# Attention scores over cached keys: one matmul against all heads, or each head in its own group of columns

## The chip, the cores and the metric

The kernel runs on one core of a Trainium2 chip. It is timed as device time in microseconds (us). One launch computes a whole inference step of a small decoder layer for two groups of tokens: 1024 prompt tokens, and 8 sample tokens, each with 256 cached keys of its own. Before the change the median of three runs is 1493.83 us (1492.7 to 1494.16).

## The reference

The layer is a mixer (four heads of differential attention beside four heads of retention, then one output projection), attention into a memory, and an MLP. The change touches one piece of the first: the differential attention of the 8 sample tokens.

```python
def probs(qi, ki):
    s = jnp.einsum('bqhd,bkhd->bhqk', qi, ki) * scale + bias
    return jax.nn.softmax(jnp.where(mask, s, neg), axis=-1)

attn = probs(q1, k1) - lam * probs(q2, k2)
return jnp.einsum('bhqk,bkhd->bqhd', attn, v)
```

A head has a query and a key of two halves of 64 (`q1`, `q2`, `k1`, `k2`), so two maps. For a sample token a map has 257 scores: 256 against its cached keys, which lie in pages of 128 keys at places that a page table names, and one against its own new key. A bias by distance, from a table of 32 rows and 4 heads, is added to each. In all there are 8 tokens x 4 heads x 2 maps = 64 rows of 257 scores. Everything is float32.

## The kernel before, in words

The program is one long list of instructions written by a Python function, `decoder_step`. A planner places it on the engines and adds the waits. Between `pin[0] = True` and `pin[0] = False`, matmuls keep the order in which the program writes them (`pinned`, `mm`, `transpose`); the other engines' order is the planner's, apart from places that name an instruction they must follow (`issue_after`, `behind`).

The stage around the change is the prompt's differential attention, head by head. A loop over `g` (line 1329), from -4 to 39, goes through ten items for each of the four heads. An item transposes a block of softmax weights (`turn`, `trA` in the trace), forms scores of one or two later blocks of 128 queries (`scores`, `sp`; the table `SCORES` says which, and `q` runs from 0 to 7), and multiplies the weights of the block before with the values (`weigh`, `av`). `scores` reads its banks with VectorE (line 1001, bias and running minimum), takes the exponential on ScalarE (line 1007) and combines the two maps on VectorE (line 1016, `e`). `turn` needs `e`, and `weigh` needs what ScalarE and VectorE made of the transpose (`ah`, `al`, lines 1034 and 1035).

Between these, other matmuls are dealt out by a generator, `filler`: `next(filler)` runs it to its next `yield`. It first yields the query and key projections of the heads to come (`head_proj`), then the sample tokens' attention (`decode_steps`). From item 28 on only the latter is left, and `DFILL` (line 2433) says how many turns of it each item from 28 to 39 takes: 1, 3, 4, 3, 1, 1, 2, 2, 1, 1, 1, 1. What is left runs out after the loop. From item 37 on, `out_ahead` adds matmuls of the output projection (`pr_o`).

`decode_steps` works so. Four of its turns are taken earlier by name (`DECODE_AT`): they load indices and constants and start the gathers of the first four of eight key tiles. A key tile (`raws2[4 * j + x]`, `ck` in the trace) is 128 partitions by 1024 columns: two tokens (`y`), four heads, 128 keys of page `j`; the partitions are the 128 elements of a key, both halves. A tile is two gathers of GpSimd's queue (`gather`, line 859). The first four tiles lie in buffers of the weight ring, the last four in the three buffers tagged `raw`, so they wait until these come free: the two from a row of factors and a block of values of the prompt's attention, and for the eighth tile that of the fifth. In the same queue item 30 puts two loads of 2 MB, `UL` and `UH` (`operand_steps`, line 1255), which the output projection needs.

The scores of one token, a step, are one matmul (line 1211): the stationary operand has 64 columns, the token's 8 queries (4 heads x 2 maps) in their own 8 columns and zeros in the others' 56; the moving operand is all 512 columns (4 heads x 128 keys) of that token. Eight tokens accumulate into one bank, 64 rows by 512 columns. Of each row only the 128 columns of its own head mean anything, so four VectorE instructions with a mask by head (line 1218, `hm`) pick them and add them to the bias rows in `SD`. The bias is a small matmul of its own (`dbias`), the own key's score another (`down`). A softmax over 257 columns follows, twelve turns that do nothing, and a matmul with `sel` that adds up the two maps (`dcomb`).

A float32 matmul shows in the trace as two weight loads and two matmuls, one for each pass.

## Time and profile before

| | before |
|---|---|
| device time, median of 3 runs | 1493.83 us |
| lowest and highest run | 1492.7, 1494.16 us |
| profiled execution | span 1492.5 us (the page gives no other time for it) |
| TensorE busy | 1474.0 us, 99% |
| VectorE, ScalarE, GpSimd busy | 1102.5, 678.4, 325.4 us |
| matmuls `dsc` (cached keys) | 32, from 397.4 to 435.7 us |

The span goes from the first instruction to the last of one profiled execution. TensorE is PE in the rows (its weight loads PEld), VectorE is DVE, ScalarE ACT, GpSimd POOL, and SP issues DMAs. Matmuls are pipelined: the duration of one is longer than the time until the next may start, so what a matmul costs is read from the start of one to the start of the next. In rows in order of time stand the start, the duration, engine, line, operation, what is written and read, the shape, how many were merged, and in square brackets how long the engine had been idle and what ended it.

### The profile page before, as it was taken

Reading aid. Unit: us, or ns where it says so; the run is one execution under the profiler, and the core shown is the slowest. Engines: PE = TensorE matmul, PEld = TensorE weight load, DVE = VectorE, ACT = ScalarE, POOL = GpSimd, SP = SyncE. Lnnn points to the kernel's source line nnn. Section 1 sums busy time; section 2 is a strip of 40 time slices with the busy share of each in tenths; the row PEclk is TensorE's granted clock in tenths of the full one; section 3 lists DMA queues with packets and bytes.
Section 4 is the critical chain, followed back from the end, with each engine's and each line's share of the span. In section 5 each row is a group of like instructions: output and inputs, shape, how many; then the busy total and the mean of one; then the engine's idle time right before and its main releaser. Section 6 shows DMA issues by size and latency. Waiting matters only on the chain.

```text
span 1492.5 us, 27826 instructions
## 1 busy us (share of the span) xinstructions
PE 1474.0 (99%) x10893; PEld 1402.5 (94%) x10893; DVE 1102.5 (74%) x2279; ACT 678.4 (45%) x1326; POOL 325.4 (22%) x346
## 2 busy tenths in 40 slices
PE   9999999998999999999999999999999999999997
PEld 7899779998769999989999999999999999999997
DVE  7656636987877734567786978888888889787875
ACT  7534435665652432147535634334344444343454
POOL 0035323114414321104132000000001311020380
PEclk9999999999999999999999999999999999999999
DMA  8155737214857157483592443344436674536273
GB/s 292 61 186 168 201 71 181 80 34 123 232 181 279 49 191 193 132 238 103 165 321 72 128 149 137 141 156 157 142 141 210 237 265 142 172 99 191 81 129 114
DMA packets 125229, 236.67 MB, mean 159 GB/s; under 512 B 13744, under 2 KB 76517, under 8 KB 124970
## 3 DMA queue, kind: packets, MB, share of 16 engines
q1 hardware_dynamic: 89056, 170.50, 36.5%
q0 software_dynamic: 24912, 44.80, 10.9%
q10 hardware_dynamic: 11130, 19.60, 3.5%
q8 instruction: 85, 1.39, 0.4%
q14 instruction: 46, 0.38, 0.1%
HBM read 170.24 MB, written 57.52 MB: 153 GB/s over the span
## 4 chain that ended last, share of the span: by engine, by line
PE 90%; DVE 5%; ACT 2%; issue 1%; DMA 1%; ACTq 0%; POOL 0%; DVEq 0%; SPq 0%
PE dn L2309 21%; PE Z L2143 9%; PE qkp L75 7%; PE pr_o L75 6%; PE mq L75 6%; PE pr_m L75 6%; PE X L2143 6%; PE Y L2143 6%; PE grp L75 3%; PE sp L75 2%; PE av L75 2%; PE mv L75 2%; PE mk L75 1%; PE mpv L75 1%; PE vap_z L522 1%
## 5 line engine op out<-in xcount | busy, mean ns | idle before, releaser
L2309 PE MATMUL dn<-UH,wd 128*128 128x258 f32 x1792 | 324.6, 283 | 0.0
L2309 PEld LDWEIGHTS dn<-UH,wd 128*128 128x128 f32 x1792 | 277.5, 189 | 0.7 <-ACT c L2410 0.2
L2309 PE MATMUL dn<-UL,wd 128*128 128x258 f32 x896 | 252.8, 282 | 0.0
L2309 PEld LDWEIGHTS dn<-UL,wd 128*128 128x128 f32 x896 | 169.0, 189 | 0.0
L2413 DVE TENSOR_TENSOR c<-c,dn 128x258 f32<-128x258 f32 x216 | 88.9, 418 | 38.5 <-PE dn L2309 36.1
L2169 ACT ACTIVATE hq<-r 128x258 f32<-128x258 f32 x128 | 53.7, 421 | 118.3 <-DVE r L2168 118.3
L2143 PE MATMUL Z<-T_h,wu 128*128 128x258 f32 x512 | 98.2, 284 | 0.0
L2143 PE MATMUL X<-UH,wu 128*128 128x258 f32 x512 | 97.4, 282 | 0.0
L2287 ACT CAST wd<-raw_d 128x512 fp32r<-128x512 f32 x96 | 58.8, 620 | 79.0 <-PE dn L2309 74.6
L1953 ACT CAST wu<-raw_up 128x512 fp32r<-128x512 f32 x96 | 59.1, 617 | 59.9 <-PE Z L2143 50.0
L2280 ACT CAST UH<-raw_h 128x1032 fp32r<-128x1032 f32 x56 | 58.7, 1056 | 53.5 <-PE dn L2309 27.7
L2143 PEld LDWEIGHTS X<-UH,wu 128*128 128x128 f32 x512 | 81.3, 188 | 0.2 <-ACT p L2194 0.2
L2143 PEld LDWEIGHTS Z<-T_h,wu 128*128 128x128 f32 x512 | 81.3, 189 | 0.0
L2180 POOL DMA_DIRECT2D HT<-ht x32 | 17.2, 538 | 292.3 <-DVE ht L2179 291.8
L2281 DVE TENSOR_TENSOR UL<-raw_h,UH 128x1032 fp32r<-128x1032 f32 x56 | 73.6, 1315 | 8.6 <-ACT UH L2280 8.6
L2288 DVE TENSOR_TENSOR wd<-raw_d,wd 128x512 fp32r<-128x512 f32 x96 | 72.2, 759 | 10.0 <-ACT wd L2287 9.9
L2143 PE MATMUL Z<-T_l,wu 128*128 128x258 f32 x256 | 72.3, 282 | 0.0
L2143 PE MATMUL X<-UL,wu 128*128 128x258 f32 x256 | 72.3, 282 | 0.0
L128 ACT CAST wh_u<-raw_u 128x1024 fp32r<-128x1024 f32 x43 | 44.6, 1047 | 54.3 <-PE mq L75 31.1
L1954 DVE TENSOR_TENSOR wu<-raw_up,wu 128x512 fp32r<-128x512 f32 x96 | 64.7, 687 | 3.5 <-ACT wu L1953 3.5
L2301 POOL TENSOR_TENSOR raw_d<-raw_d,raw_d 128x512 f32<-128x512 f32 x16 | 22.1, 1383 | 193.8 <-DVE raw_d L2297 172.9
L129 DVE TENSOR_TENSOR wl_u<-raw_u,wh_u 128x1024 fp32r<-128x1024 f32 x39 | 49.4, 1273 | 18.8 <-ACT wh_u L128 18.6
(597 smaller groups left out, 4732.8 us busy)
## 6 DMA issues: line engine op xcount, KB each, us to landing
raw_u<-in_wall SPq DMA_DIRECT2D x49, 512.0 KB
HT<-ht POOLq DMA_DIRECT2D x32, 516.0 KB
raw_h<-HT SPq DMA_DIRECT2D x32, 516.0 KB
raw_up<-in_wall SPq DMA_DIRECT2D x32, 512.0 KB
raw_d<-in_wall SPq DMA_DIRECT2D x32, 512.0 KB
HQ<-hq ACTq DMA_DIRECT2D x32, 387.0 KB
raw_h<-HQ SPq DMA_DIRECT2D x24, 516.0 KB
cmk<-in_cmk SPq DMA_DIRECT2D x16, 512.0 KB
```

The source lines that it names most:

```text
L75: pinned(nc.tensor.matmul(out, l, r, start=start, stop=stop))
L129: (lo_engine or nc.vector).tensor_sub(wl[:, :n], raw[:, :n], wh[:, :n].bitcast(F32))
L1953: nc.scalar.copy(w[:, :512], src)
L1954: nc.vector.tensor_sub(w[:, 512:], src, w[:, :512].bitcast(F32))
L2143: pinned(nc.tensor.matmul(ps, l, r[:, k, :], start=first and k == 0 and x == 0, stop=k == 3 and x == 2, skip_group_check=True))
L2169: nc.scalar.activation(h[:, PLACE[quad], :], r, AF.Square)
L2280: nc.scalar.copy(h, rv)
L2281: nc.vector.tensor_sub(l, rv, h.bitcast(F32))
L2287: nc.scalar.copy(w[:, :512], src)
L2288: nc.vector.tensor_sub(w[:, 512:], src, w[:, :512].bitcast(F32))
L2309: pinned(nc.tensor.matmul(ps, l, r[:, k, cq], start=first and k == 0 and x == 0, stop=k == 3 and x == 2, skip_group_check=True))
L2413: nc.vector.tensor_add(y, y, ps)
```

## The change

Each head now gets a matmul of its own. The 128 rows of one PSUM bank are split into four groups of 32, one for each head; a head's 16 columns (2 maps x 8 tokens) are the stationary operand, and its own 128 keys the moving one. The bank holds 257 columns, as many as a row has scores, and stays open from the first to the last matmul: a bias matmul starts it with half the bias, the own key's product goes into column 256, the eight tiles into columns 0 to 255, and a second bias matmul with the other half closes it. The softmax reads the bank itself. The steps `dec_bias`, the four masked instructions for each page and `hm` are gone, and `sel` and the mark of the second map lie in the tile `qk`. A `yield` now follows each tile instead of each token.

```diff
-            sel = A.tile([64, 32], F32, tag="sel", name="sel")
-            nc.sync.dma_start(sel, i["sel"])
-            hm = A.tile([64, 5], F32, tag="hm", name="hm")
-            nc.sync.dma_start(hm, i["hm"])
...
+            nc.vector.tensor_scalar(relw, relb.unsqueeze(2).to_broadcast([32, 4, 32]), 0.5, None, ALU.mult)
...
-            nc.gpsimd.memset(qx, 0.0)
+            prod = qk[:, 512:640]
+            nc.gpsimd.memset(qk[:, 0:640], 0.0)
...
+                nc.vector.tensor_mul(
+                    prod[ms].rearrange("p (h c) -> p h c", h=4)[:, :, 8 * m : 8 * m + 8], qdec[ms], kdec[ms])
...
+            sel, second = qk[:, 900:932], qk[:, 932:933]
+            nc.sync.dma_start(qk[:, 900:933], i["sel"])
...
-            def dec_bias():
-                bp = dt("dbias")
-                mm(bp[:64, :257], rel64, oneh, True, True)
-                nc.scalar.copy(SD[:, :257], bp[:64, :257])
-                yield
-                bp = dt("down")
-                for m in range(2):
-                    ms = slice(64 * m, 64 * m + 64)
-                    mm(bp[32 * m : 32 * m + 32, :1], prod[ms], ones[ms], True, True)
-                nc.vector.tensor_add(SD[:, 256:257], SD[:, 256:257], bp[:64, :1])
-                yield
+            sp = dt("dsc")
+            mm(sp[:, :257], relw.rearrange("p h c -> p (h c)"), oneh, True, False)
+            mm(sp[:, 256:257], prod, ones, False, False)
+            yield
 
             for j in range(2):
-                sp = dt(f"dsc_{j}")
                 for x in range(4):
                     raw = raws2[4 * j + x]
-                    if (j, x) == (0, 2):
-                        yield from dec_bias()
                     for y in range(2):
                         q = 2 * x + y
-                        mm(sp[:64, :], qx[:, q * 64 : q * 64 + 64], raw[:, y * 512 : y * 512 + 512], q == 0, q == 7)
-                        yield
+                        for h in range(4):
+                            pinned(nc.tensor.matmul(
+                                sp[32 * h : 32 * h + 16, j * P : j * P + P],
+                                qx[:, q * 64 + 16 * h : q * 64 + 16 * h + 16],
+                                raw[:, y * 512 + h * P : y * 512 + h * P + P],
+                                start=False, stop=False, skip_group_check=True))
+                    yield
 
                     if 4 * j + x in (0, 1, 2, 4):
                         fetch(4 + (0, 1, 2, 0, 3)[4 * j + x])
-                sd = SD[:, j * P : j * P + P]
-                for h in range(4):
-                    nc.vector.scalar_tensor_tensor(sd, sp[:64, h * P : h * P + P], hm[:, h : h + 1], sd, ALU.mult, ALU.add)
+            mm(sp[:, :257], relw.rearrange("p h c -> p (h c)"), oneh, False, True)
-            nc.vector.tensor_reduce(mn[:, 0:1], SD[:, :257], AX.X, ALU.min)
-            nc.scalar.activation(SD[:, :257], SD[:, :257], AF.Exp, bias=mn[:, 0:1], scale=-1.0, accum_out=mn[:, 1:2])
+            nc.vector.tensor_reduce(mn[:, 0:1], sp[:, :257], AX.X, ALU.min)
+            nc.scalar.activation(SD[:, :257], sp[:, :257], AF.Exp, bias=mn[:, 0:1], scale=-1.0, accum_out=mn[:, 1:2])
```

More of the change, by code (lines that the diff above doesn't have):

```diff
@@ L1186, in decode_steps @@
             nc.sync.dma_start(oneh, i["onehot_dec"])
[L1187 removed]
+            sel, second = qk[:, 900:932], qk[:, 932:933]
+            nc.sync.dma_start(qk[:, 900:933], i["sel"])
+            SD = A.tile([P, 260], F32, tag="SD", name="SD")
             yield
[L1191 to L1201 removed]
+            sp = dt("dsc")
@@ L1223, in decode_steps @@
+            mn = A.tile([P, 4], F32, tag="dmn", name="dmn")
+            nc.vector.tensor_reduce(mn[:, 0:1], sp[:, :257], AX.X, ALU.min)
+            nc.scalar.activation(SD[:, :257], sp[:, :257], AF.Exp, bias=mn[:, 0:1], scale=-1.0, accum_out=mn[:, 1:2])
             nc.vector.reciprocal(mn[:, 1:2], mn[:, 1:2])
-            nc.vector.tensor_scalar(mn[:, 2:3], nlam[:64], 1.0, None, ALU.subtract)
-            nc.vector.tensor_scalar(mn[:, 2:3], mn[:, 2:3], hm[:, 4:5], 1.0, ALU.mult, ALU.add)
+            nc.vector.tensor_scalar(mn[:, 2:3], nlam, 1.0, None, ALU.subtract)
@@ L1226, in decode_steps @@
+            nc.vector.tensor_scalar(mn[:, 2:3], mn[:, 2:3], second, 1.0, ALU.mult, ALU.add)
             nc.vector.tensor_mul(mn[:, 1:2], mn[:, 1:2], mn[:, 2:3])
```

26 lines of the change are left out of this document (9 added, 17 removed).

## The prediction

> **What bounds the kernel now.** I read the page first, then the busy times by stretch around the change, then the time-ordered rows of each engine there.
>
> ```profile
> span 1492.5 us, 27826 instructions
> PE 90%; DVE 5%; ACT 2%; issue 1%; DMA 1%; ACTq 0%; POOL 0%; DVEq 0%; SPq 0%
> ```
>
> The chain that ended last is TensorE for 90% of the span, so TensorE time taken out moves the end, wherever nothing else waits in its place. The page gives no device time for the profiled execution, only its span of 1492.5; I make the sum in the span's own clock. The median of the three timed runs, 1493.83, lies 1.3 above the span, and I add the change to that median. Busy time in a stretch where the cached keys are used, and in one behind it:
>
> ```profile
> 405.00:410.00 5.00, 5.00 (x24) 2.57 (x22) 4.30 (x14) 3.03 (x7) 1.54 (x4) 1.00 1.09 417
> 440.00:470.00 30.00, 30.00 (x190) 28.41 (x189) 15.12 (x32) 9.02 (x15) 7.69 (x6) 1.00 0.55 186
> ```
>
> After the length come the busy times of TensorE, its weight loads, VectorE (DVE), ScalarE and GpSimd, the clock, the DMA share and GB/s. Where the keys are used, VectorE is busy for 4.30 us of 5 and DMA for the whole time: TensorE leads by little, and two others stand close behind. Behind it, VectorE has half its time free. TensorE's own order, in start times (items are the values of `g` in the loop over the last head):
>
> ```profile
> 400.34 1.07 PE L75 MATMUL dsc<-ck,qblkd 128*64 128x512 f32 x2
> 401.35 0.39 PE L75 MATMUL av<-ah,VH 128*128 128x256 f32 x1
> 401.57 0.28 PE L75 MATMUL av<-al,VH 128*128 128x256 f32 x1
> 401.69 0.28 PE L75 MATMUL av<-ah,VL 128*128 128x256 f32 x1
> ...
> 406.68 0.64 PE L75 MATMUL dbias<-qblkd,rel 32*64 32x257 f32 x2
> 407.25 0.39 PE L75 MATMUL av<-ah,VH 128*128 128x256 f32 x1
> ...
> 408.15 0.23 PE L75 MATMUL down<-ones,qblkd 64*32 64x1 f32 x4
> 408.31 0.44 PE L75 MATMUL sp<-KA,Q 128*128 128x384 f32 x1
> ...
> 410.20 0.55 PE L78 MATMUL trA<-ident,e 128*128 128x128 f32 x3
> ...
> 411.68 0.47 PE L75 MATMUL sp<-KA,Q 128*128 128x448 f32 x1
> ...
> 427.11 0.55 PE L78 MATMUL trA<-ident,e 128*128 128x128 f32 x3 [0.38 <-DVE e L1016]
> ...
> 437.01 0.32 PE L75 MATMUL pr_o<-UH,wh_u 128*128 128x344 f32 x1
> ```
>
> Three marks carry the sum: 410.20, where item 31 begins; 427.11, the transpose that waits for the last prompt softmax (VectorE L1016); 437.01, the first output-projection matmul. Behind the third TensorE has ready work without a gap (the second row: busy for 30.00 of 30.00), so a shift there goes on to the end.
>
> **The matmuls.** One step (one of 16 rounds of a 512-column matmul in its two passes) takes 401.35 − 400.34 = 1.01 us. Sixteen are 16.2; the bias 407.25 − 406.68 = 0.57, the own key 408.31 − 408.15 = 0.16: 16.9 us go. In their place each key tile gets 2 rounds x 4 heads of 128 columns, two passes each. A pass of 512 columns is 1.01 / 2 = 0.50, of 128 columns 0.126. Side by side in four column groups, a tile is 2 x 2 x 0.126 = 0.5; the first step after a change of tile shape is 0.22 (401.35 to 401.57) against 0.12 for the next (to 401.69), so with 0.1 for that 0.6 us, eight tiles 4.8. Without overlap it is 16 x 0.126 + 0.1 = 2.1, eight tiles 16.8. No four column groups run in this trace; the nearest row is the own key, on two tiles of different rows and columns: four matmuls in 0.16 us, though each lasts far longer, and
>
> ```profile
> 408.15 0.19 PE L75 MATMUL down<-ones,qblkd 64*32 64x1 f32 x2
> 400.34 0.19 PEld L75 LDWEIGHTS dsc<-ck,qblkd 128*64 128x64 f32 x2 [0.19 <-issue]
> ```
>
> two of them lie within 0.19 us together, that is on top of each other (the first row is the answer for 408.155 to 408.203). I take 0.6, and keep 2.1 as the other end. The bias is now added twice, 1.14, the own key about 0.2 as before. Matmuls: 6.1 instead of 16.9, so 10.8 us less; without overlap 1.2 more. [...] The trace speaks against it: the two loads in the second row, on the same rows, are done in 0.19 us, while the first matmul, begun with the first load, runs for half a us.
>
> **Where the work stands.** The steps between yields get fewer: before, each 512-column step is one turn of the filler; now a whole tile is one, and bias and own key together are one. Items 28 to 39 still take 1, 3, 4, 3, 1, 1, 2, 2, 1, 1, 1, 1 turns (`DFILL`). So item 29 takes bias and tiles 0, 1; item 30 tiles 2 to 5; item 31 tiles 6, 7, the second bias and the softmax; items 32 to 37, which had 8 of the 16 steps, take none. The 10.8 us come out of the later items, while the need for tiles 4 to 7 moves forward from items 32 to 37 into items 30 and 31. TensorE's order is pinned: what waits for tile 6 holds up every score, transpose and value matmul behind it.
>
> **When the tiles land.** GpSimd issues, and DMA rate from 391 to 417 in 40 slices of 0.65 us:
>
> ```profile
> 400.68 0.82 POOL L1255 DMA_DIRECT2D UH<-OPH  x1
> 403.74 1.64 POOL L977 TENSOR_TENSOR VL<-vraw,VH 128x512 fp32r<-128x512 f32 x1 [2.24 <-ACT VH L975]
> ...
> 409.19 1.00 POOL L859 DMA_INDIRECT ck<-in_cache_kT,idk  x1 [0.51 <-POOL al L1033]
> 410.49 0.95 POOL L859 DMA_INDIRECT ck<-in_cache_kT,idk  x1 [0.30 <-issue]
> GB/s 139 180 251 330 298 197 227 157 209 167 297 380 419 419 413 393 386 392 405 405 411 405 404 404 410 424 413 432 432 426 432 406 406 386 341 139 25 25 0 0
> ```
>
> The gather of tile 6 (two issues, 409.19 and 410.49) stands in GpSimd's queue behind the load of UH; the bytes stop at 391 + 38 x 0.65 = 415.7. Its buffer is that of `vraw_3`, free once VL is made (403.74 + 1.64 = 405.4), so it can be issued 4 us sooner. That doesn't help: UH went out at 400.68, the rate is full until 413.7, and the same bytes stand ahead of it. Tile 6 is there at about 416, tile 7, two more gathers of 128 rows by 512 floats, 256 KB each, at some 0.4 MB per us, at 417.3.
>
> **Forward from item 31.** Items 29 and 30 hold 6 tiles, one bias and the own key, 3.6 + 0.8 = 4.4, where 5 steps, bias and own key took 5.8; their scores and transposes wait for VectorE, so I leave item 31 at 410.2, up to 1 sooner. Its transposes end at 410.7; tile 6 is due, and TensorE stands until about 416.0, 5.3 us. The scores of block 6 start at 416.6 instead of 411.68: 4.9 late. VectorE then has this to do until its last L1016:
>
> ```profile
> 412.40 0.62 DVE L1001 CUSTOM_DVE_ANT_0 e<-sp,M 128x448 f32<-128x448 f32 x1 [0.41 <-PE sp L75]
> ...
> 425.76 1.29 DVE L1016 SCALAR_TENSOR_TENSOR e<-e,mn,e 128x1024 f32<-128x1024 f32 x1
> L1218 DVE SCALAR_TENSOR_TENSOR SD<-dsc,hm,SD 64x128 f32<-64x128 f32 x4 | 1.3, 334 | 0.7 <-PE dsc L75 0.7
> 440.79 0.41 DVE L1220 TENSOR_REDUCE dmn<-SD 64x1 f32<-64x257 f32 x1
> ```
>
> 412.40 to 427.05 is 14.65. The four L1218 go (1.3) with the 0.7 waited for them; some 1.3 of it, block 5's L1016 (the row's 1.29 is that of the widest), gets done during TensorE's stand; the decode softmax comes in, its reduction 0.41 and three small ones, 1.1 at most. That leaves 12.4: from 416.6 + 0.7 to 429.7, so 427.11 becomes 429.7, 2.6 late. From there 9.9 us follow before, with 4 steps, 4.0, that are gone. TensorE alone would take 5.9; but VectorE has
>
> ```profile
> L129 DVE TENSOR_TENSOR wl_u<-raw_o,wh_u 128x1024 fp32r<-128x1024 f32 x3 | 3.7, 1221 | 0.0
> L145 DVE SCALAR_TENSOR_TENSOR UL<-op,subln,UH 128x1024 fp32r<-128x1024 f32 x2 | 2.6, 1282 | 0.2 <-ACT UH L144 0.2
> L1035 DVE TENSOR_TENSOR al<-trA,ah 128x512 fp32r<-128x512 f32 x3 | 2.1, 685 | 0.0
> ```
>
> (427.1 to 437.0), and ahead of the second L1035, which the value matmuls before 437.01 need, stand three L129, one L145 and one L1035: 3.7 + 1.3 + 0.7 = 5.7, with two small ones and that L1035 itself some 6.7, with the value matmuls behind it 7.6 in all. 429.7 + 7.6 = 437.3, or 436.1 if the third L129 falls behind it. I take 436.5, nearer the second, since VectorE's order is planned anew with less TensorE work in these items, against 437.01: 0.5 us earlier. Moved DMAs: `sel` now goes out on SP behind the one-hot rows, and the early loads of `sel` and `hm` are gone; nothing is queued close behind them. The four loads of output weights wait for the scores to end and come some 3 us later; they have until 437. All else in the diff (the wider memset, two products for one, a dropped copy on ScalarE) is under 0.3 us each on engines with room.
>
> **Forecast:** 1493.83 − 0.5 = 1493.3, own range 1490.8 to 1496.5: 2.5 less if both the third L129 falls behind and the tiles land a us sooner, 3 more if VectorE's order, which is planned anew, puts the decode softmax or the late `sel` in a prompt block's way.
>
> **Rivals.**
> *1. No stand.* If tile 6 is issued ahead of UH, it lands behind tile 5, by 411, and block 6 starts at 411.4. VectorE then bounds: 14.65 − 1.3 − 0.7 − 0.9 of waits on scores + 1.1 = 12.9 from 412.1, ends 425.0, plus 7.6 is 432.6: 4.4 earlier, less 0.4 for a partial wait, 1489.8. For it: the gather's place in the program moves from item 31 into item 30, ahead of both loads. Against: before, UL went out ahead of tile 5's gather though it stands behind it in the program, because the buffer wasn't free; tile 6's buffer frees later still.
> *2. Column groups in line: slower.* At 2.1 a tile, seven tiles, a bias and the own key (15.5) replace six steps, bias and own key (6.8) up to block 6's scores: 411.68 + 8.7, block 6 at 420, with nothing left to wait for from DMA. VectorE: 420.0 + 0.7 + 12.4 = 433.1, plus 7.6: 440.7, 3.7 late, 1497.5. It decides from some 1.5 us a tile, where TensorE reaches tile 6 after it has landed (410.7 + 6 x 0.9 = 416.1). Against it stand the two rows of overlap; for it, that no row has the same rows in four groups.
> *3. Clock falls in the stand.* Here the clock is 1.00 through waits as long as
>
> ```profile
> 359.87 0.55 PE L78 MATMUL trA<-ident,e 128*128 128x128 f32 x3 [2.03 <-DVE e L1016]
> 1486.00:1489.00 3.00, 0.00 (x0) 0.00 (x0) 2.37 (x4) 0.00 (x0) 0.00 (x0) 0.50 0.50 166
> ```
>
> 2.03 us, and 0.50 once TensorE is done at the end. 5.3 us lies between. At half clock for the first 3 us of work after it, block 6's and 5's work is up to 1.5 later: 1493.3 + 1.5 = 1494.8. [...]
>
> **Chances.** Forecast 0.48, rival 1 0.24, rival 2 0.18, rival 3 0.10. A change under 0.2%, 3 us, can't be told from none. Within it lie 0.41 of the forecast's 0.48 (0.04 faster, 0.03 slower), 0.02 of rival 1, 0.03 of rival 2 and 0.08 of rival 3: same 0.54, faster 0.04 + 0.22 = 0.26, slower 0.03 + 0.15 + 0.02 = 0.20. The range, 1488.5 to 1498.3, takes in rivals 1 and 2 up to a us beyond their values.
>
> **What would show it.** Weight loads of four heads starting a few ns apart, and a tile in 0.6 us, against 2.1; a TensorE wait of 4 to 6 us ahead of tile 6 that the gather ends; granted clock in that stretch; the 427.11 transpose 2 to 3 us later while the first output matmul is not. It is wrong if there is no such wait, or if the order of VectorE has changed so that the last L1016 ends before 427.

## The result, and the profile after

The change makes the kernel slower: 1501.07 us median (1500.1 to 1501.88, four runs) against 1493.59 (1492.7 to 1494.16, four runs), a ratio of 1.0046 with a 95% interval of 1.0032 to 1.0060. The profiled execution took 1500.1 us; its span is 1498.3, which is 5.8 more than the span before. From the page of the changed kernel, the granted clock in 40 slices (in tenths, 9 for 90% or more) and the share of the chain that ended last:

```profile
PEclk9999999999989999999999999999999999999999
...
PE 89%; DVE 5%; DMA 2%; issue 2%; ACT 2%; POOL 0%; another core or an unknown queue 0%; SPq 0%; DVEq 0%; ACTq 0%; POOLq 0%
```

TensorE is still the chain, for 89% instead of 90%, and one slice shows that its clock was not whole. TensorE's rows of the stage, in order of time (start, duration, operation, what it writes and reads, and in brackets the idle time before it and what ended it):

```profile
395.40 0.44 PE L78 MATMUL trA<-ident,e 128*128 128x128 f32 x2 [0.18 <-DVE e L1016]
396.15 0.70 PE L75 MATMUL dsc<-qblkd,relw 32*128 32x257 f32 x2 [0.31 <-DMA qblkd<-in_onehot_dec]
397.51 0.35 PE L75 MATMUL dsc<-ones,qblkd 128*128 128x1 f32 x2 [0.67 <-issue]
...
401.75 0.63 PE L1198 MATMUL dsc<-ck,qblkd 128*16 128x128 f32 x16
402.31 0.41 PE L75 MATMUL sp<-KA,Q 128*128 128x320 f32 x1
...
414.69 0.41 PE L1198 MATMUL dsc<-ck,qblkd 128*16 128x128 f32 x8 [3.60 <-issue]
415.33 0.63 PE L1198 MATMUL dsc<-ck,qblkd 128*16 128x128 f32 x8 [0.23 <-DMA ck<-in_cache_kT,idk]
415.89 0.74 PE L75 MATMUL sp<-KA,Q 128*128 128x448 f32 x1
...
426.24 0.39 PE L75 MATMUL av<-ah,VH 128*128 128x256 f32 x1 [0.58 <-ACT ah L1034]
427.57 0.39 PE L75 MATMUL av<-al,VH 128*128 128x256 f32 x1 [0.95 <-DVE al L1035]
...
430.02 0.90 PE L78 MATMUL trA<-ident,e 128*128 128x128 f32 x3 [1.48 <-DVE e L1016]
...
432.00 3.41 PE L75 MATMUL ct<-ones,sq 128*128 128x1 f32 x16
...
439.43 0.32 PE L75 MATMUL pr_o<-UH,wh_u 128*128 128x344 f32 x1
```

A tile (two tokens, four heads) takes 402.31 − 401.75 = 0.56 us where two steps took 2.0. TensorE stands 3.60 + 0.23 us ahead of tile 6 (for the 3.60 the profile names no releaser; in run e6 below the same wait, 3.35 us, ends with the tile's DMA). The transpose that waits for the last prompt softmax comes at 430.02, the first output-projection matmul at 439.43. To compare profiles whose time has drifted before the stage, I count from the first row, a pair of transposes at the entrance of the stage, which stood at 396.94 before:

```profile
396.94 0.44 PE L78 MATMUL trA<-ident,e 128*128 128x128 f32 x2 [0.18 <-DVE e L1016]
```

| us from the entrance of the stage | before | changed | later by |
|---|---|---|---|
| scores of block 6 | 14.74 (411.68) | 20.49 (415.89) | 5.75 |
| last-softmax transpose | 30.17 (427.11) | 34.62 (430.02) | 4.45 |
| first output-projection matmul | 40.07 (437.01) | 44.03 (439.43) | 3.96 |
| end of the span | 1095.6 | 1102.9 | 7.4 |

So the stage costs 4.0 us and what lies behind it another 3.4; 1.5 are the drift ahead of the stage (396.94 − 395.40), and 4.0 + 3.4 − 1.5 = 5.8. Busy times of TensorE (first column after the length), its weight loads, VectorE, ScalarE and GpSimd, then the granted clock, the DMA share and GB/s, in stretches of 3.4 us that follow the changes of the clock:

```profile
394.60:398.00 3.40, 2.11 (x10) 1.01 (x8) 3.26 (x10) 1.56 (x7) 0.99 (x1) 0.99 1.13 323
398.00:401.40 3.40, 3.38 (x24) 2.44 (x25) 3.40 (x14) 2.13 (x6) 1.78 (x2) 0.51 1.14 407
401.40:404.80 3.40, 1.88 (x25) 1.26 (x23) 1.94 (x4) 2.23 (x5) 1.26 (x1) 1.00 1.06 400
...
411.60:415.00 3.40, 0.31 (x8) 0.13 (x8) 1.96 (x4) 1.40 (x3) 2.33 (x5) 1.00 0.89 285
415.00:418.40 3.40, 3.17 (x32) 1.80 (x28) 1.22 (x3) 0.00 (x0) 0.00 (x0) 0.50 0.63 180
...
425.20:428.70 3.50, 1.81 (x12) 1.14 (x10) 3.33 (x10) 3.12 (x7) 0.56 (x3) 1.00 0.88 317
428.70:432.10 3.40, 2.08 (x11) 2.09 (x11) 3.15 (x3) 2.89 (x4) 0.00 (x0) 0.50 0.33 134
432.10:435.50 3.40, 3.40 (x18) 3.40 (x18) 1.19 (x3) 3.21 (x4) 0.00 (x0) 0.50 0.53 159
435.50:438.90 3.40, 3.40 (x16) 3.20 (x16) 3.40 (x6) 2.00 (x3) 1.99 (x1) 0.50 0.01 2
```

Three times TensorE is busy for 2.11, 0.31 and 1.81 us of a stretch, and each time the next stretch runs at half clock. Only one of the three holds the long stand. After the last, the clock stays halved for 10.2 us, through a stretch with more waiting (2.08 busy) and one that is full, but mostly with the sixteen one-column `ct` matmuls (432.00, 3.41 us). A small busy share alone doesn't decide: the stretch from 401.40 was busy for 1.88 us, less than the 2.11 of the first, and the clock stayed whole behind it (1.00 from 404.80 to 408.20). In the MLP, some 750 us on, where each engine's order of work is as before, two waits stand that weren't there, and behind the second the clock is halved once more:

```profile
1164.52 0.39 PE L2298 MATMUL dn<-UH,wd 128*128 128x258 f32 x1 [0.67 <-ACT c L2399]
...
1212.54 0.36 PE L2298 MATMUL dn<-UH,wd 128*128 128x258 f32 x1 [1.77 <-DVE c L2402]
...
1213.80:1217.20 3.40, 3.40 (x18) 3.40 (x17) 1.73 (x5) 0.81 (x1) 0.00 (x0) 0.51 1.07 355
```

The two waits are 2.4 us, and 3.4 us at half clock cost up to 1.7; together they cover the 3.4 that came on top behind the stage. (A halved stretch of 3.4 us also lies ahead of the stage, from 353.6.)

### The profile page after: what moved, and what is told of

It is laid out like the page before. It is cut to its first block, busy times and chain, and to the rows that moved or that the text cites. A ratio compares the mean times of both kernels' runs of the same rounds, so it can differ in the third digit from the quotient of the medians.

```text
span 1498.3 us, 28001 instructions
## 1 busy us (share of the span) xinstructions
PE 1472.1 (98%) x10989; PEld 1411.6 (94%) x10989; DVE 1100.5 (73%) x2270; ACT 678.0 (45%) x1325; POOL 319.7 (21%) x346
## 4 chain that ended last, share of the span: by engine, by line
PE 89%; DVE 5%; DMA 2%; issue 2%; ACT 2%; POOL 0%; another core or an unknown queue 0%; SPq 0%; DVEq 0%; ACTq 0%; POOLq 0%
PE dn L2298 19%; PE Z L2132 9%; PE qkp L75 7%; PE pr_m L75 6%; PE pr_o L75 6%; PE mq L75 6%; PE X L2132 6%; PE Y L2132 6%; PE grp L75 3%; PE sp L75 2%; PE av L75 2%; PE mv L75 1%; PE mk L75 1%; PE mpv L75 1%; PE vap_z L522 1%
## 5 line engine op out<-in xcount | busy, mean ns | idle before, releaser
L2269 ACT CAST UH<-raw_h 128x1032 fp32r<-128x1032 f32 x56 | 58.7, 1055 | 54.8 <-PE dn L2298 28.3
L2277 DVE TENSOR_TENSOR wd<-raw_d,wd 128x512 fp32r<-128x512 f32 x96 | 72.1, 757 | 10.3 <-ACT wd L2276 10.2
L1007 ACT ACTIVATE e<-e,mn 128x128 f32<-128x128 f32 (+6 forms) x64 | 49.7, 777 | 30.5 <-DVE mn L1001 26.7
```

The costliest lines, as they stand in the source:

```text
L1007: nc.scalar.activation(e[:, :n], e[:, :n], AF.Exp, bias=mn[:, m : m + 1], scale=-1.0, accum_out=sm[:, m, q : q + 1])
L2269: nc.scalar.copy(h, rv)
L2277: nc.vector.tensor_sub(w[:, 512:], src, w[:, :512].bitcast(F32))
```

## The experiments

The changed kernel has two new things: narrow matmuls (N), and a turn for each tile (T) where there was one for each token. I had two explanations. Theory A, a guess from the three stretches of 2.11, 0.31 and 1.81 us above: the loss is the halved clock, which falls wherever a stretch holds too little matmul work. The rival: it is the stand ahead of tile 6, and VectorE's work behind it; the clock only fills waits. Comparisons were made on different occasions, on which the kernel before itself took between 1489.9 and 1495.1 us, so only ratios are carried from one to another. "Stage" is the time from the entrance transposes to the first output-projection matmul, "behind" from there to the end of the span, "half" how long the clock was halved within the stage (in whole stretches of 3.4 us), all of the one profiled execution.

| kernel | stage | half | behind | ratio and 95% interval |
|---|---|---|---|---|
| before | 40.07 | 0 | 1055.5 | 1 |
| before again (e8) | 40.08 | 0 | 1055.3 | 1.0002 [0.9993, 1.0012] |
| changed | 44.03 | 17.0 | 1058.9 | 1.0046 [1.0032, 1.0060] |
| changed again (e7) | 44.01 | 17.0 | 1056.3 | 1.0040 [1.0027, 1.0052] |
| e1: N without T | 34.58 | 0 | 1057.4 | 0.9995 [0.9979, 1.0011] |
| e4: T without N | 44.93 | 10.2 | 1054.8 | 1.0039 [1.0025, 1.0053] |
| e2: loads behind the last gather | 46.89 | 23.8 | 1057.6 | 1.0055 [1.0038, 1.0072] |
| e3: eight added matmuls of 1 us | 49.54 | 13.6 | 1059.3 | 1.0068 [1.0051, 1.0084] |
| e5: tiles 6, 7 later | 38.64 | 13.6 | 1056.9 | 0.9993 [0.9980, 1.0006] |
| e6: two added in item 34 | 44.15 | 13.6 | 1056.3 | 1.0022 [1.0012, 1.0032] |
| e9: N without T, own key later | 39.30 | 10.2 | 1056.1 | 0.9995 [0.9980, 1.0010] |
| e10: the same, three added | 36.80 | 3.4 | 1057.6 | 0.9996 [0.9987, 1.0005] |
| e15: N without T, waits filled | 38.22 | 10.2 | 1055.8 | 0.9988 [0.9977, 0.9999] |
| e16: the same, front filled too | 34.56 | 0 | 1059.4 | 0.9966 [0.9953, 0.9979] |
| e17: changed, waits filled | 40.44 | 3.4 | 1055.4 | 0.9995 [0.9986, 1.0004] |

**The change in two halves (e1, e4).** e1 keeps the narrow matmuls and gives each token its turn again:

```diff
                                 start=False, stop=False, skip_group_check=True))
-                    yield
+                        yield
```

> The changed kernel with the matmuls by column group, but with a yield after each token again, so that tiles 6 and 7 are needed from item 34 on, as before the change. Theory A (the loss is TensorE's halved clock, which falls where a window holds little matmul work): the 4 us stand ahead of tile 6 is gone, but items 29 to 37 still have 10.8 us less of matmul work between waits for VectorE, so the clock falls in one or two places and the time is 1493 to 1498. Rival B (the loss is the stand ahead of tile 6 and the clock costs little by itself): 1489 to 1492, faster than before the change.

e4 keeps the wide matmuls of before, with a turn for each tile:

```diff
                         mm(sp[:64, :], qx[:, q * 64 : q * 64 + 64], raw[:, y * 512 : y * 512 + 512], q == 0, q == 7)
-                        yield
+                    yield
```

> The kernel before with its own 512-column matmuls, but with the yield after each tile instead of after each token: the regrouping of turns alone. Tiles cost 2.0 us, so TensorE reaches tile 6 at about 417, when it has landed. Theory A (halved clock): dense work until item 31, then five items without filler, where the clock falls once VectorE bounds: 1496 to 1500. Rival B (the stand ahead of tile 6): no stand, 1494 to 1496.

e1 is no slower than before (0.9995), e4 nearly as slow as the whole change (1.0039). So the turns, which look like a detail of it, carry the loss. For e1 theory A had named 1493 to 1498, the rival 1489 to 1492; the median was 1488.79, with the kernel before at 1489.87 beside it. TensorE's rows of e1, then of e4:

```profile
393.05 0.44 PE L78 MATMUL trA<-ident,e 128*128 128x128 f32 x2 [0.18 <-DVE e L1016]
...
400.23 0.55 PE L78 MATMUL trA<-ident,e 128*128 128x128 f32 x3 [0.91 <-DVE e L1016]
...
410.51 0.55 PE L78 MATMUL trA<-ident,e 128*128 128x128 f32 x3 [1.14 <-DVE e L1016]
...
419.71 0.55 PE L78 MATMUL trA<-ident,e 128*128 128x128 f32 x3 [1.16 <-DVE e L1016]
...
427.63 0.32 PE L75 MATMUL pr_o<-UH,wh_u 128*128 128x344 f32 x1
```

```profile
392.51 0.44 PE L78 MATMUL trA<-ident,e 128*128 128x128 f32 x2 [0.18 <-DVE e L1016]
...
411.49 0.47 PE L75 MATMUL sp<-KA,Q 128*128 128x448 f32 x1
...
425.71 0.39 PE L75 MATMUL av<-al,VH 128*128 128x256 f32 x1 [2.43 <-DVE al L1035]
...
428.15 0.90 PE L78 MATMUL trA<-ident,e 128*128 128x128 f32 x3 [1.20 <-DVE e L1016]
...
437.44 0.32 PE L75 MATMUL pr_o<-UH,wh_u 128*128 128x344 f32 x1
```

e1's stage is 5.5 us shorter than before's: the 10.8 us taken from TensorE are half a gain, then TensorE waits for VectorE, 0.91, 1.14 and 1.16 us. In e4 the long steps stand ahead of block 6's scores (18.98 from the entrance, 4.2 late), the last-softmax transpose is 5.5 late (35.64), and work moved forward leaves holes behind it (2.43, then 1.20); behind the first the clock falls, at 426.2. e1's ten runs lie far apart, 1484.5 to 1495.2, and the mean clock goes with them: 0.998 in the shortest, 0.992 and 0.993 in the two longest. The profile, with no fall, shows one of the good ones; the 5.5 us aren't in the median.

**The stand (e2, e5).** e2 holds the loads of `UL` and `UH` back until the last gather has been issued:

```diff
+                    seen["G"] = nc.cur_bb.bb.instructions[-1]
...
+                with tc.issue_after(seen["G"]):
-                nc.gpsimd.dma_start(dst[:, 4:8, :], part[:, :, :].rearrange("k p c -> p k c"))
+                    nc.gpsimd.dma_start(dst[:, 4:8, :], part[:, :, :].rearrange("k p c -> p k c"))
```

> The changed kernel with the two 2 MB loads of UL and UH (line 1255) held in GpSimd's queue until the last gather of a key tile has been issued. Both theories: tile 6 lands by about 411, and the scores of block 6 begin near 411.5 instead of 415.9. Theory A (halved clock): the falls near 398 and 428 stay, 1495 to 1498. Rival B (the stand): 1490 to 1493.

TensorE's rows of e2:

```profile
407.87 0.97 PE L1199 MATMUL dsc<-ck,qblkd 128*16 128x128 f32 x16
...
410.57 0.41 PE L1199 MATMUL dsc<-ck,qblkd 128*16 128x128 f32 x8 [0.74 <-DMA ck<-in_cache_kT,idk]
414.23 0.41 PE L1199 MATMUL dsc<-ck,qblkd 128*16 128x128 f32 x8 [3.24 <-DMA ck<-in_cache_kT,idk]
```

Tile 6 is ready, without a wait, and block 6's scores come 16.72 us after the entrance, as both theories expected; but TensorE now stands 0.74 + 3.24 us for tile 7. Its gathers went out behind tile 4, at 406.46 and 407.72, and the second was there only at 414.23, with the loads of `UH` and `UL` issued right behind it; whether these slowed it was not tested. The stand moved on by a tile, and the clock was halved for longer. The ratio, 1.0055, lies above what either theory named (1495 to 1498 us, or 1490 to 1493). e5 instead uses tiles 6 and 7 later, in item 34, with five of the twelve empty turns moved ahead of them:

```diff
                 for x in range(4):
+                    for _ in range(5 if (j, x) == (1, 2) else 0):
+                        yield
                     raw = raws2[4 * j + x]
...
-            for _ in range(12):
+            for _ in range(7):
```

> The changed kernel, with five of its twelve empty turns moved from behind the scores to the place ahead of tile 6: tiles 6 and 7 are used in item 34 instead of item 31, when their gathers have landed, and the softmax over the cached keys follows in item 35. TensorE's work and every transfer stay as they are. Theory S (the loss of the changed kernel is the stand ahead of tile 6, 3.6 + 0.23 us, which sets back every prompt softmax behind it, with the halved clock that it leaves): no wait over 2 us on TensorE in this stage, block 6's scores some 17.5 us after the bias matmul's start instead of 19.7 (396.15 to 415.89), the first output-projection matmul some 33 to 36 us after it instead of 43.3, the time 1.002 to 0.994 of the kernel before. Rival C (TensorE has too little to do in this stage wherever the tiles stand, the clock falls anyway): the stand goes but the clock falls to half for 10 us as before, the time 1.002 to 1.005 of the kernel before.

No wait for a tile is left, and 5.4 us of the stage are gone. Each theory got one thing right: with the stand the loss goes (0.9993, theory S), but the clock is halved all the same, for 13.6 us (rival C), and the first output-projection matmul comes 38.0 us after the bias matmul (393.87 to 431.90), not 33 to 36. Both this and e1 undo the need for tiles 6 and 7 in item 31, and each alone undoes the loss. Neither is measurably faster than before.

**The clock (e3, e6, e10).** e3 adds a matmul of 512 columns, two passes, about 1.0 us, in each of the first eight empty turns; its result is read by nothing:

```diff
+            wp = dt("dwarm")
-            for _ in range(12):
+            for n in range(12):
+                if n < 8:
+                    mm(wp[:64, :], qx[:, :64], qx, True, True)
                 yield
```

> The changed kernel with a 512-column float32 matmul of 1.0 us, whose result nothing reads, in the first eight of the twelve empty turns, so that items 32 to 37 hold the same amount of matmul work as before the change: 8.1 us more work on TensorE. Theory A (halved clock): the 10.2 us at half clock from 428.7 on are gone, and since these items wait for VectorE anyway, the time falls by 2 to 5, to 1496 to 1499. Rival B (the clock costs little): 8 us more work on the engine that bounds, 1503 to 1509.

The `ct` matmuls run at full clock (1.95 us), but the stage is 5.5 us longer than the changed kernel's: most of the eight us don't fall into waits and add to the path, and behind the stand the clock was halved for 10.2 us in this execution. The ratio is the rival's number (1503 to 1509 us), not theory A's (1496 to 1499). A fill as coarse as this can't tell the two explanations apart. e6 adds only the fourth and fifth of them (`if n in (3, 4)`), both in item 34, sized to its waits:

> The changed kernel, with two unread matmuls of 512 columns (two passes each, about 1.0 us) in the two turns of item 34, where TensorE stands 0.58 + 0.95 us ahead of the value matmuls and then 1.48 us ahead of the transpose of the last prompt softmax; nothing is added elsewhere, and the stand ahead of tile 6 stays. If the halved clock from 428.7 to 438.9 is what keeps the first output-projection matmul at 439.4 (theory A): the clock stays at 1.0 there, the sixteen ct matmuls take 1.8 us instead of 3.3, that matmul comes 2 to 3 us sooner, and the time is 1.002 to 1.004 of the kernel before. If VectorE bounds there and the clock only fills its waits (rival V): the clock stays up, ct takes 1.8, but the first output-projection matmul is less than 1 us sooner or even later, the time 1.004 to 1.007.

The ratio is as theory A gave it, 1.0022 beside 1.0040 for the changed kernel on the same occasion (e7). The profile shows why it isn't more. TensorE's rows of e6, with the answer by stretches between them:

```profile
392.09 0.44 PE L78 MATMUL trA<-ident,e 128*128 128x128 f32 x2 [0.18 <-DVE e L1016]
...
429.26 0.55 PE L78 MATMUL trA<-ident,e 128*128 128x128 f32 x3 [0.34 <-DVE e L1016]
...
436.24 0.32 PE L75 MATMUL pr_o<-UH,wh_u 128*128 128x344 f32 x1
```

```profile
407.40:410.80 3.40, 0.65 (x11) 0.31 (x3) 2.33 (x6) 1.40 (x3) 2.49 (x3) 1.00 0.89 310
410.80:421.10 10.30, 9.69 (x54) 6.42 (x55) 3.47 (x12) 1.88 (x5) 1.43 (x3) 0.50 0.52 157
```

From the last-softmax transpose to the output projection 6.98 us pass instead of 9.41: that is the 2 to 3 us. But in this execution 10.2 us of halved clock followed the stand, where 3.4 had followed it, and that transpose came 37.17 us after the entrance instead of 34.62. e9 moves the own key's matmul behind tile 1, since TensorE waited for its operand at the front:

```diff
-            mm(sp[:, 256:257], prod, ones, False, False)
...
                     raw = raws2[4 * j + x]
+                    if (j, x) == (0, 2):
+                        mm(sp[:, 256:257], prod, ones, False, False)
```

> The narrow matmuls with a turn after each token, as in the run with the old turns, and the own key's matmul moved from the front, where TensorE stood 0.86 us for its operand (395.16 there), to the place behind tile 1, as in the kernel before. Theory A (TensorE's clock falls by chance of where its windows lie, wherever a window holds little work; that is why the runs with the old turns lie between 1484.5 and 1495.2): one such place is gone, the median falls by 1 to 2 us, 0.997 to 0.999 of the kernel before, and some runs still lose 5 us or more. Rival V (VectorE bounds the stage, the wait at the front is hidden, and the spread has nothing to do with it): the median and spread stay, 0.999 to 1.001.

```profile
395.89 0.42 PE L75 MATMUL sp<-KA,Q 128*128 128x320 f32 x1 [1.31 <-DVE mn L1001]
```

The wait stays and has another owner: VectorE's L1001. Rival V was right here, nothing is gained. e10 adds three unread 1.0 us matmuls to e9, with three of the tokens, ahead of the scores and the transposes that wait:

```diff
+                        if (4 * j + x, y) in ((0, 1), (4, 0), (6, 0)):
+                            mm(wp[:64, :], qx[:, :64], qx, True, True)
                         yield
```

> The kernel with the own key later and, beside it, three unread matmuls of 512 columns (about 1.0 us each), put with the second token of tile 0 and the first tokens of tiles 4 and 6, ahead of the three transposes for which TensorE stood 0.91, 1.14 and 1.16 us with the old turns (400.23, 410.51, 419.71). Theory A: the waits shrink to under 0.5 us, the clock stays at 1.0 through the stage in nearly all runs, the first output-projection matmul stays where it was in the undisturbed run with the old turns (34.0 us after the bias matmul) or up to 1 us later, the spread of the runs shrinks to 4 us or less, and the median is 0.996 to 0.998 of the kernel before. Rival V: the added matmuls push scores back that VectorE needs, the first output-projection matmul comes 2 to 3 us later, and the time is 0.999 or above.

The spread falls from 13.1 us (e9) to 3.6, as theory A said, but the stage is 2.2 us longer than e1's, and the ratio stays at 0.9996. 1.05 us of it are there at the last-softmax transpose (27.71 from the entrance, 26.66 in e1), while the clock was still whole: the fill also pushed back scores that VectorE needs. The rest came with 3.4 us of halved clock from 424.6, which followed a stretch in which TensorE was busy for all of 3.40 us, with the `ct` matmuls in it.

**The waits alone filled (e15, e16, e17).** What was missing is a fill that can't push anything back. These kernels use a one-pass matmul (0.23 us) with operands that are there already, unread too, and place it straight ahead of the instruction that waits:

```diff
+                def turn_on(g=g):
+                    for _ in range({30: 3, 32: 4, 35: 4}.get(g, 0)):
+                        mm(seen["W"][:, :], ...)
+                    turn(*items[g + 1])
-                todo.append(lambda: turn(*items[g + 1]))
+                todo.append(turn_on)
```

That is e15, on top of e1; e16 adds three between the bias and the own key's matmul. e17 puts them into the waits of the changed kernel: three at the front, thirteen ahead of tile 6, six and five ahead of the transposes of items 30 and 35, two behind that of item 34.

> The narrow matmuls with the old turns, and unread matmuls of 512 columns in one pass (0.23 us each, with operands that are there already) straight ahead of the three transposes for which TensorE stood 0.91, 1.14 and 1.16 us: three, four and four of them, so that they fit into the waits. Theory A: the clock stays at 1.0 through the stage in nearly all runs, the first output-projection matmul 34.0 us after the bias matmul (within 0.5), the median 1486 to 1488 where the kernel before has 1491, 0.997 to 0.998, runs within 5 us of each other. Rival V (the spread comes from somewhere else than this stage's clock): the spread stays at 8 us or more and the median at 0.999 to 1.000.

> The same with three more of these matmuls between the bias matmul and the own key's, where TensorE stood 0.86 us. Theory A: as the one before or up to 1 us better, since the front was one of the places where the clock fell (394 to 401 in other profiles), no fall before 1470, 0.9965 to 0.998. Rival V: 0.999 to 1.000, spread as before.

> The changed kernel with the same unread matmuls of 0.23 us in its waits alone: three at the front, six ahead of the transpose that waited 1.82 us, thirteen (3.0 us) ahead of tile 6, for which TensorE stood 3.4, two and five in the waits of items 34 and 35 (0.58 + 0.95 and 1.48 us). Theory A (the halved clock sets the loss behind the stand, as far as the prediction missed it): no halved clock in the stage, block 6's scores still 4 to 5 us late, the last-softmax transpose 2 to 3 us late, the first output-projection matmul within 1 us of the kernel before in place of 3.9 us late, the time 1.001 to 1.002. Rival V (VectorE's later order bounds it, the clock only fills its waits): the clock stays up, but that matmul is still 2.5 us late or more, 1.003 to 1.005.

TensorE's rows of e17, then of e16:

```profile
396.06 0.44 PE L78 MATMUL trA<-ident,e 128*128 128x128 f32 x2 [0.18 <-DVE e L1016]
...
410.38 3.24 PE L75 MATMUL dwarm<-Q 128*128 128x512 f32 x13
415.28 0.41 PE L1207 MATMUL dsc<-ck,qblkd 128*16 128x128 f32 x8 [1.67 <-DMA ck<-in_cache_kT,idk]
...
416.27 0.47 PE L75 MATMUL sp<-KA,Q 128*128 128x448 f32 x1
...
429.28 0.55 PE L78 MATMUL trA<-ident,e 128*128 128x128 f32 x3 [0.31 <-DVE e L1016]
...
430.37 1.84 PE L75 MATMUL ct<-ones,sq 128*128 128x1 f32 x16
...
436.50 0.32 PE L75 MATMUL pr_o<-UH,wh_u 128*128 128x344 f32 x1
```

```profile
397.46 0.44 PE L78 MATMUL trA<-ident,e 128*128 128x128 f32 x2 [0.18 <-DVE e L1016]
...
432.02 0.32 PE L75 MATMUL pr_o<-UH,wh_u 128*128 128x344 f32 x1
```

In e17 TensorE still can't go on before tile 6 has landed: block 6 stands at 20.21 from the entrance, 0.3 sooner than in the changed kernel. But the stage is 40.44 instead of 44.03, 0.4 over before's, and the ratio is 0.9995 instead of 1.004: filling the waits gives back 3.6 us, and 0.4 are left for the stand, all that it moves, and 3.4 us of halved clock that remained (from 432.7). In the stage theory A holds. The ratio goes beyond its numbers, and 3.6 us of stage are only half of what the ratio gained. e16 is the same test on the other side: no halved clock in the stage, which is as short as in e1's profiled execution, 34.56, and a median of 1490.81 us (1488.53 to 1493.16) beside 1495.10 for the kernel before, 0.9966 [0.9953, 0.9979]; a fall behind the stage, from 783.5, was not forecast. With the front left open (e15) the clock fell from 398.3 to 405.2, behind a wait of 0.89 us, the first output-projection matmul came 37.7 us after the bias matmul and not 34.0, and the ratio is 0.9988, between the two theories. On this occasion the kernel before itself took longer, at a mean clock of 0.995 to 0.998 where it had 0.997 to 0.999 beside e1 to e14, and neither e1 nor the changed kernel ran beside it; so how much of the two ratios is the filling, and how much the occasion, is not shown beyond the 0.0022 between e15 and e16. The price of the turns is plain too, with 3.4 us of halved clock left in e17: 40.44 − 34.56 = 5.9 us.

**Four groups of columns (e14).** Only head 0's matmuls are issued (`for h in range(1)`), so three heads' scores are left out of the sample tokens' attention.

> The changed kernel with the matmuls of one head only for the cached keys; three heads' scores are left out, so the attention of the sample tokens is not the reference's. If four column groups run side by side (as the prediction took it): a tile with one head takes about as long as with four, 0.45 to 0.56 us, and TensorE's place at the marks of the stage changes by less than 0.5 us. If the four stand in line, a tile takes 0.15 to 0.2. For the MLP: if the 96 more TensorE instructions of the narrow matmuls shift something that its loads run into, the waits for c are gone; if not, they stay at 0.6 us or more.

```profile
401.96 0.61 PE L1198 MATMUL dsc<-ck,qblkd 128*16 128x128 f32 x4
402.50 0.45 PE L75 MATMUL sp<-KA,Q 128*128 128x384 f32 x1
```

One head takes 0.54 us, four take 0.56: the other three cost 0.02. And less work made nothing faster (1.0040 [1.0026, 1.0055]); the clock was halved for about 20 us of this stage.

**The MLP (e11, e12, e13, and the repeats).** e11 puts the constant `hm` and its load back into the changed kernel, unread; e12 gives the kernel before an unread constant of 7424 bytes, by which the constants had grown; e13 gives the changed kernel one that makes the growth 65536.

> The changed kernel with the constant hm and its early load put back, unread, so that as many transfers and constants are there as in the kernel before. In the changed kernel TensorE stands 0.6 us and more for c in the MLP, where the kernel before does not, with the same order of work on every engine; the loads of raw_h that VectorE needs there land 0.5 to 1 us later. If the missing transfer (which queue or place the later transfers get) is the cause: those waits go, and the time is 1.5 to 2 us below the changed kernel's, 1.0025 to 1.003 of the kernel before. If not: the waits stay, 1.004 to 1.005.

> The kernel before with one more constant of 7424 bytes that nothing reads, as much as the constants grew in the changed kernel, so that what follows in memory can lie as there. If the place in memory is what makes the loads of raw_h late in the MLP: TensorE waits for c in the MLP of 0.6 us or more, 1.001 to 1.0015 of the kernel before. If not: no such wait, 1.000.

> The changed kernel with one more constant, unread, of 58112 bytes, which with the growth of sel makes 65536, so that what follows lies a round distance from where it lay before. If the place in memory decides: the MLP's waits for c go and the time is 1.002 to 1.003 of the kernel before. If not: waits of 0.6 us and more, 1.004 to 1.005.

> The changed kernel unaltered, beside the others on one chip. Its halved clock and its waits of 0.67 and 1.77 us in the MLP (at 1164.5 and 1212.5) belong to the kernel if they come again: 1.004 to 1.006 of the kernel before, a stage up to the first output-projection matmul 43 us after the bias matmul, waits for c in the MLP of 1.5 us or more together. If the MLP's waits were chance, they are below 0.5 us together and the time is 1.002 to 1.003.

> The kernel before unaltered, for a profile on this chip: ratio 1.000, clock 1.0 through the stage from 390 to 440 and through the MLP, no wait for c in the MLP over 0.3 us if those waits come with the change; waits of 0.5 us or more there if they come and go by themselves.

Putting the transfer back or moving the place in memory didn't take the waits away: e11 took 1.0053 [1.0039, 1.0066] with a wait of 1.55 us at 1211.8, e13 1.0043 [1.0027, 1.0060] with 0.47 and 0.80, e12 0.9996 [0.9986, 1.0005] with a wait of 0.58. The changed kernel again (e7) had 0.58 and 0.52, the kernel before (e8) none. One head alone (e14) has none either, and that is the outcome it named for the 96 additional TensorE matmuls as the cause: it issues as many as the kernel before. In the fourteen profiles with all 128 narrow matmuls the waits for `c` of 0.25 us and more add up to 0.65 to 2.68 us; in the five with 32 matmuls for the cached keys (before, e4, e8, e12, e14) e12's 0.58 is the only one. So they go with the number of matmuls rather than with their shape, as far as one or two profiles of each kernel can tell; by what way the number acts stays open.

A second part is the clock. Seven of the nineteen profiles have a halved stretch of 3.4 us behind the stage (the changed kernel from 1213.7; e2, e3, e11, e12, e14 and e16 between 783 and 796); they take 1056.5 to 1059.4 us there, the other twelve 1054.8 to 1057.6. The four longest, 1058.9 to 1059.4 (changed, e3, e11, e16), have both: waits of over 2.2 us and a halved stretch. Behind the stage the four profiles with wide matmuls (before, e4, e8, e12) take 1054.8 to 1057.1 us, the fifteen with narrow ones 1055.4 to 1059.4; the means lie 1.6 us apart, but the ranges overlap, and the changed kernel's 1058.9 was 1056.3 when it ran again, without a halved stretch behind the stage. So of the 3.4 us a part comes and goes from one execution to the next.

## Why the prediction was wrong

**The matmuls: right.** 0.6 us a tile was taken, 0.56 measured, and e14 shows that the groups overlap almost wholly: 0.56 us for four heads, 0.54 for one. Rival 2, at 2.1 a tile, is out.

**The stand: right in place and time, its cause not separated.** 5.3 us were forecast, with tile 6 at 416.0; its first half came at 414.69, in an execution that entered the stage 1.54 earlier, so at 416.2 on the scale of before. The wait was shorter (3.83) because TensorE itself arrived later, through two other waits (0.67 us, and 1.82 at 405.10) and a halved clock. The prediction let the gather of tile 6 go out 4 us sooner and named the bytes ahead of it as the limit; in the run it went out at 409.44, which is 1.8 later than before on the same scale, when a matmul of the cached keys had ended. How much of the stand is that late issue and how much the bytes of `UH`, no run separates. Block 6's scores were to be 4.9 late and were 5.75, or 5.5 in e17, at full clock. Rival 1 is out: tile 6 was gathered behind `UH` (issued at 399.13), and e2, which turns that order round, only moves the stand to tile 7.

**VectorE's share: right at full clock, not as it ran.** From block 6's scores to the last-softmax transpose the sum was 13.1 us (416.6 to 429.7). e17 took 13.0 (416.27 to 429.28), the changed kernel 14.1 (415.89 to 430.02): scores at half clock (0.50 from 415.00 to 418.40) reach VectorE later.

**The tail: the step that failed.** "429.7 + 7.6 = 437.3, or 436.1 [...] I take 436.5 [...] against 437.01: 0.5 us earlier." The 6.8 us between the two marks were made of durations from a profile whose clock was 1.00. The changed kernel took 9.41, because the clock was halved from 428.7 to 438.9: the `ct` matmuls alone took 3.3 us instead of 1.8. e17 took 7.2, e6 7.0, between the two values from which I chose (6.4 and 7.6). With the clock held up but for 3.4 us (e17) the steps of the sum are met within 0.6 us, and its end within 0.9 (0.4 later instead of 0.5 earlier). In the stage, the error is the clock. (A slip of no weight: the upper end of the sum's own range, 1493.3 + 3, is 1496.3 and not 1496.5.)

**Rival 3 named the right cause, in one place of three and at too low a price.** It asked how long one wait must be, put the limit between 2.03 and 5.3 us, granted one fall, behind the stand, of about 3 us, and priced it 1.5. No run shows that length; behind the stand the clock was halved for 3.4 us in the changed kernel and for 10.2 in e6. But the first fall followed waits of 0.18, 0.31, 0.67 with a bias matmul between them, the third, and dearest, waits of 0.58 and 0.95 us. The length of one wait, then, isn't what decides; most falls followed a stretch of 3.4 us in which TensorE did little (busy for 0.31 to 2.11 us ahead of the three in the changed kernel's stage, 0.65 ahead of the one behind e6's stand), but neither is the busy share the whole rule (no fall behind 1.88 us at 401.40, one behind 3.40 us in e10), and what it is stays open. Taking 10.8 us of work out of a stage whose other engines set the pace left such stretches. That was to be seen: VectorE was busy 4.30 us of 5 in the row that the prediction quotes, so a good part of the time saved had to become waits. The halved stretches last 3.4, 6.8 or 10.2 us, and kernels with the same work in the stage differ in them (17.0 us in the changed kernel, 20.4 in e11 and e13). That the falls depend on where windows lie, as theory A has it for e9, was my estimate, and no run shows it.

**The turns were priced only through tile 6.** The prediction followed the regrouping to the stand, but compared it with the kernel before, and not with the narrow matmuls in the old turns. Those would have been 5.5 us ahead in the stage at full clock; the sum hid a gain of 5.5 behind a loss of 5.9 (e17 against e16, 3.4 us of e17 at half clock).

**Behind the stage, a second step that failed.** The prediction carried the shift on to the end, since TensorE had "ready work without a gap"; the row for that covers 30 us of the 1055 that follow. In the profiled execution 3.4 us came on top: two waits for `c` in the MLP (2.4 us together) and 3.4 us of halved clock behind them. The halved stretch wasn't there when the kernel ran again, and of the waits 1.1 us were left.

## What to carry to other kernels

Of the 10.8 us of work taken from TensorE here, where VectorE nearly kept up with it (busy for 4.30 us of 5 before), 5.5 shortened the stage of e1, and the rest turned into waits; in the changed kernel the waits had a second price, 17.0 us of halved clock, of which 3.4 were left when they were filled (e17): look at how much work is left in every few us of such a stage, and not only at the longest wait, and check the sum's durations against the clock that will then be granted. A change of the matmuls and a change of the order in which they are dealt out should be timed apart; here one was worth 5.5 us in its stage at full clock and the other cost 5.9. Where TensorE waits anyway, matmuls that nobody reads, no longer than the wait and straight ahead of what waits, held the clock through the stage (e16: 0.9966, against 0.9988 beside it with one wait left open, and 0.9995 without any on another occasion); longer ones, put a turn earlier, cost what they brought or more (e10: 0.9996 beside 0.9995 in e9; e3: 1.0068 where the changed kernel had 1.0046 and 1.0040).

## What the runs showed of the hardware

- The granted clock fell after stretches in which TensorE was busy for 2.11, 0.31 and 1.81 us of 3.4, and didn't come back after a stretch that showed it busy for all of 3.40 with sixteen one-column matmuls in it. The busy share is not the rule by itself: behind 1.88 us (401.40 in the changed kernel) the clock stayed, behind 3.40 us with the `ct` matmuls (421.20 in e10) it fell. Coming back took one stretch (busy 3.38 or 3.17 us at half clock) in the changed kernel and three in e6, the second of them busy for all of 3.40.
- Behind the same stand of 3.4 to 3.8 us the clock was halved for 3.4 us in two profiles of the changed kernel and for 10.2 in that of e6. The runs of one kernel differ by up to 13 us (e9: 1484.81 to 1497.90), and the mean clock goes with them (0.998 and 0.988), while the kernel before, at full clock through the stage in both its profiles, stayed within 5.2 (its 23 runs beside e16).
- Four groups of 16 columns, each with all 128 rows, ran in 0.56 us (402.31 − 401.75, changed kernel) where one alone took 0.54 (402.50 − 401.96, e14), in float32.
